# A Fourier mixer on folded tokens and channels: projecting, transforming and projecting back the even and the odd part separately

## The chip, the cores and the metric

The kernel runs on one core of a Trainium2 chip. The metric is the device time of one execution in microseconds. A core has five engines with their own instruction streams: TensorE (PE; matmuls, with weight loads shown as PEld), VectorE (DVE), ScalarE (ACT), GpSimd (POOL) and SyncE (SP, which issues most DMAs). Matmuls read SBUF and write PSUM; PSUM has eight banks of 512 fp32 columns.

## What is computed

One step of a small diffusion backbone with two layers. 512 latent tokens (a grid of 8 rows by 64 columns) and 128 context tokens, of 1024 channels each, share the weights. Each layer is a half-step SwiGLU feed-forward, a token mixer and a second half-step feed-forward, each wrapped in RMSNorm before and after, with shift, scale and gate from a modulation (`W_mod`) of a condition vector. The mixer of layer 1 is attention. The mixer of layer 0, which the change is about, is

```
def _fourier_mix(h, w_in, w_out):
    b, s, _ = h.shape
    u = (h @ w_in).reshape(b, s, N_FOURIER_GROUPS, FOURIER_GROUP_DIM)      # 8 groups of 128 channels
    f = jnp.fft.fft2(u.astype(jnp.float32), axes=(1, 3), norm="ortho").real
    return f.astype(h.dtype).reshape(b, s, D_MODEL) @ w_out
```

taken over the 512 latent tokens and over the 128 context tokens as two sequences. The real part of a two-dimensional transform is cosine times cosine minus sine times sine. A cosine sees only the even part of its input, the sum of a token (or channel) and its mirror image, and a sine only the odd part, the difference.

## The kernel before, in words

All matrices are fp32. A product is made of three matmuls (`mm3`, L233): each operand is split into a rounded part "hi" and a rest "lo" (`split`, L220: a copy on ACT, L222, and a subtraction on DVE, L223), and hi·hi, hi·lo and lo·hi are summed in PSUM (L236 to L238). Every weight unit, 128 x 1024, is loaded by SP into one of four "raw" buffers, split by ACT and DVE into one of six "hi"/"lo" pairs or into "ring" blocks, and used by PE; `unit` (L175) sends units three ahead of the one that is asked for.

The work is a sequence of six sub-layers n = 0 to 5. Feed-forward n = 0 (`ffn`, L624) goes over 22 hidden blocks in five slices: for each slice a w1 part (320-column matmuls over the two token halves) and a w2 part (512-column matmuls for five token tiles of 128, accumulated in PSUM and parked in SBUF between slices). In the last slice w2 runs over tiles (0, 1), then 2, then (3, 4). After a tile's last matmul `chain` (L567) does its post-norm, gate and residual (L576 to L586), the next pre-norm (L595 to L603), and then, a set number of modelled PE nanoseconds later (the number that the first `yield` hands out), eight PE transposes into channel-major form (L608), the scale and shift (L617 on ACT, L619 on DVE) and the split into the next layer's hidden state. The context is tile 4.

The modulation weights of later sub-layers are worked off in the background: 128 jobs, each one raw load and two DVE multiply-and-sum operations (L432). The list `BEHIND` says how many of them stand behind the w2 parts of each feed-forward (36 for n = 0); 12 jobs stand in the Fourier layer, six behind its input projection and six behind its output projection.

The Fourier layer (`fourier`, L964), n = 1:

- input projection: for each token half (320 tokens) eight output blocks of 128 channels times eight contraction chunks, `multi` (L273), copied into y channel-major (L1011);
- `fold` (L974, DVE): tokens and their mirror images are added and subtracted along the free axis;
- `channels` (L1018): per group of 128 channels, plain fp32 matmuls with the 128 x 128 cosine and sine matrices (L1026 to L1030), result split;
- `positions` (L1037): per group, three-matmul products with the 256-row position matrices (256 or 258 columns), then the unfolding of even and odd sums (L1049 to L1055) and a split;
- `out_proj` (L946): tiles (0, 1), then 2, then (3, 4), each tile two 512-column halves times eight chunks; tiles 0, 1 and 3 in the four "main" banks, tiles 2 and 4 in the two "score" banks. After each group the chains of its tiles start.

PSUM is handed out by tag: four "main" banks, two "score", one "turn", one "sum". A bank comes free when the last reader of its former tile is done.

## Time and profile before

| | us |
|---|---|
| median of 3 runs (lowest to highest) | 2217.96 (2216.83 to 2218.72) |
| profiled execution | 2217.38 |
| its span, first to last instruction | 2215.6 |
| PE busy in it | 2186.6 |
| DVE busy | 1724.0 |
| ACT busy | 1171.5 |
| POOL busy | 42.8 |

The rest of the profiled execution's time, 1.8 us, lies around the span. The page's groups name the line, the engine, the operation, "out<-in" by tile names, the shape, the count, and after the bar the busy time, the mean duration of one and the idle time of the engine just before it, with what ended that idle time. The view by stretches gives the same busy times for windows of the span. The timeline lists instructions in order of time with start and duration.

### The profile page before, as it was taken

To read this page: it belongs to the slowest core of one execution; us is meant where nothing else is said; L and a number is where in the kernel's file an instruction comes from. 1 tells how busy PE (TensorE), PEld (TensorE's weight loads), DVE (VectorE), ACT (ScalarE), POOL (GpSimd) and SP (SyncE) were. 2 spreads that over 40 slices of the span, in tenths; PEclk is the share of its full clock that TensorE was granted. 3 is DMA by queue.
4 is the path that set the end of the run, shared out by engine and by line. 5 is a ranking of instruction groups with operands and counts; after the bars stand their busy time and mean duration, and the time that the engine had idled before them with its cause. 6 is when DMAs were issued, how large, how long until landed. Compare 5 with 4: busy or idle time off the path is not lost. (4 is left out here: it accounts for less than half of the span.)

```text
span 2215.6 us, 35198 instructions
## 1 busy us (share of the span) xinstructions
PE 2186.6 (99%) x13646; PEld 2039.2 (92%) x13646; DVE 1724.0 (78%) x3158; ACT 1171.5 (53%) x2207; POOL 42.8 (2%) x95
## 2 busy tenths in 40 slices
PE   7999999999999999999999999999999999999998
PEld 5999998999899998998999999989999899999997
DVE  5988898687888898887988898786555686766684
ACT  4544544464454454455544554466778654455452
POOL 0000000000000000000000000000000000000000
PEclk9999999999999999999999999999999999999999
DMA  8244344533424444444244344523343322322232
GB/s 315 86 143 162 134 152 135 189 118 100 157 89 150 136 141 145 159 144 168 90 145 158 126 148 149 199 82 107 104 120 110 104 95 99 113 95 87 95 126 103
DMA packets 85575, 292.33 MB, mean 132 GB/s; under 512 B 9664, under 2 KB 14624, under 8 KB 85280
## 3 DMA queue, kind: packets, MB, share of 16 engines
q1 hardware_dynamic: 84864, 289.43, 38.9%
q8 instruction: 107, 1.75, 0.3%
q10 hardware_dynamic: 544, 0.66, 0.1%
q14 instruction: 60, 0.49, 0.1%
HBM read 274.53 MB, written 11.58 MB: 129 GB/s over the span
## 5 line engine op out<-in xcount | busy, mean ns | idle before, releaser
L222 ACT ACTIVATE hi<-raw 128x1024 fp32r<-128x1024 f32 (+1 forms) x387 | 369.2, 967 | 297.7 <-PE score L237 85.0
L223 DVE TENSOR_TENSOR lo<-raw,hi 128x1024 fp32r<-128x1024 f32 (+1 forms) x387 | 427.9, 1112 | 103.4 <-ACT hi L222 102.0
L236 PE MATMUL main<-hi,ring 128*128 128x512 f32 (+2 forms) x1044 | 391.9, 376 | 1.8 <-ACT ring L1338 1.8
L432 DVE SCALAR_TENSOR_TENSOR junk<-raw,wide 128x1024 bf16<-128x1024 f32 x256 | 313.2, 1223 | 97.1 <-DMA raw<-in_w_mod_t 92.5
L237 PE MATMUL main<-lo,ring 128*128 128x512 f32 (+2 forms) x1044 | 387.6, 371 | 0.8 <-DVE lo L223 0.8
L238 PE MATMUL main<-hi,ring 128*128 128x512 f32 (+2 forms) x1044 | 387.2, 371 | 0.0
L238 PE MATMUL score<-ring,lo 128*128 128x320 f32 x916 | 283.5, 309 | 0.8 <-DVE lo L223 0.6
L236 PE MATMUL score<-ring,hi 128*128 128x320 f32 x916 | 283.6, 310 | 0.0
L237 PE MATMUL score<-ring,hi 128*128 128x320 f32 x916 | 283.0, 309 | 0.0
L236 PEld LDWEIGHTS main<-hi,ring 128*128 128x128 f32 x1044 | 196.3, 188 | 36.7 <-ACT ring L1338 2.2
L238 PEld LDWEIGHTS main<-hi,ring 128*128 128x128 f32 x1044 | 196.0, 188 | 34.3 <-issue 0.2
L237 PEld LDWEIGHTS main<-lo,ring 128*128 128x128 f32 x1044 | 196.3, 188 | 33.4 <-DVE lo L223 1.1
L236 PE MATMUL turn<-ring,hi 128*128 128x320 f32 x680 | 210.8, 310 | 2.5 <-DVE left L760 2.5
L236 PE MATMUL sum<-ring,hi 128*128 128x320 f32 x680 | 210.4, 309 | 0.3 <-DVE left L764 0.3
L238 PE MATMUL turn<-ring,lo 128*128 128x320 f32 x680 | 210.1, 309 | 0.0
L237 PE MATMUL sum<-ring,hi 128*128 128x320 f32 x680 | 210.1, 309 | 0.0
L238 PE MATMUL sum<-ring,lo 128*128 128x320 f32 x680 | 210.1, 309 | 0.0
L237 PE MATMUL turn<-ring,hi 128*128 128x320 f32 x680 | 210.1, 309 | 0.0
L824 ACT ACTIVATE y<-main 128x512 f32<-128x512 f32 x160 | 94.1, 591 | 198.4 <-PE main L238 197.4
L236 PE MATMUL main<-ring,hi 128*128 128x320 f32 x560 | 181.5, 324 | 2.0 <-ACT ring L222 1.6
L238 PE MATMUL main<-ring,lo 128*128 128x320 f32 x560 | 175.1, 313 | 1.7 <-DVE lo L223 1.7
L237 PE MATMUL main<-ring,hi 128*128 128x320 f32 x560 | 174.9, 312 | 0.8 <-DVE ring L223 0.8
(253 smaller groups left out, 4292.5 us busy)
## 6 DMA issues: line engine op xcount, KB each, us to landing
raw<-in_w SPq DMA_DIRECT2D x272, 512.0 KB, 3.8
raw<-in_w_mod_t SPq DMA_DIRECT2D x128, 512.0 KB, 3.5
raw<-in_qkv SPq DMA_DIRECT2D x26, 512.0 KB, 3.7
spill<-ring SPq DMA_DIRECT2D x12, 640.0 KB, 3.0
ring<-spill SPq DMA_DIRECT2D x12, 640.0 KB, 6.7
raw<-in_bias SPq DMA_DIRECT2D x16, 448.0 KB, 3.5
first<-in_w_mod_k SPq DMA_DIRECT2D x8, 512.0 KB, 8.0
ring<-in_w_mod_k SPq DMA_DIRECT2D x8, 512.0 KB, 10.2
```

Of the source, the lines that this page charges most:

```text
L222: a = self.nc.scalar.activation(hi, src, AF.Copy)
L223: self.last_split = a, self.nc.vector.tensor_tensor(lo, src, hi.bitcast(F32), op=ALU.subtract)
L236: mm(out, whi, xhi, start=start, stop=False)
L237: mm(out, whi, xlo, start=False, stop=False)
L238: self.latest = mm(out, wlo, xhi, start=False, stop=stop)
L432: last = self.nc.vector.scalar_tensor_tensor(out=self.junk, in0=raw, scalar=1.0, in1=self.wide[:, cond, :], op0=ALU.mult, op1=ALU.mult, ac ...
L824: nc.scalar.activation(place(i, a), ps[a], AF.Copy)
```

## The change

**Token order.** The host puts latent tokens and their mirror images into two tiles at the same rows: tiles 0 and 1 are a pair, tiles 3 and 4 are a pair, and the context becomes tile 2, in the order 0 to 64, then 127 down to 65. Input, outputs, bias, cache outputs and the column ranges in attention (`QUERY_SEGS`, `KEY_SEGS`, `ATT_SPAN`, `ATT_COLS`, `OUT_COLS`) follow it; attention's token halves become 256 and 384 columns.

**Folding.** In `chain` of n = 0 the two tiles of a pair are replaced by sum and difference before the transposes, which are done for both at once; the context tile is folded after them. The input projection's weights are folded over channels and the output projection's over channels when a unit is sent (`send`, kinds `fold` and `foldrows`).

**Fourier layer.** Input projection token-major: even tokens against even channels (2 x 260 columns), odd tokens against odd channels (504 columns); then positions (`sums`, `diffs`), then channels (with two groups in one 128 x 128 block matrix), then the output projection of even and odd part, added and subtracted into the two tiles of a pair. The order of the output is pair (0, 1), tile 2, pair (3, 4).

**Schedule.** `BEHIND` for n = 0 is 48 instead of 36, and the 12 jobs in the Fourier layer are gone. The delays before transposes for n = 0 are a list of their own. In feed-forward 0 the last slice takes tiles 3 and 4 one after the other, and tile 4 no longer starts in fresh "score" banks.

The diff, cut to its core:

```diff
-BEHIND = (36, 12, 36, 36, 0, 8)
+BEHIND = (48, 0, 36, 36, 0, 8)
+TURNS = (
+    {0: 10500, 1: 14000, 2: 9200, 3: 11000, 4: 13000},
+    {1: 15500, 2: 9200, 4: 12500},
+)
...
+        elif kind.startswith("fold"):
+            raw = self.raw_tile(src)
+            a, b = raw[:, one], raw[:, two]
...
+            nc.vector.tensor_tensor(b, a, b, op=ALU.subtract)
+            for x, y in [(a, b)] if "rows" in kind else [(a[:, i], b[:, i]) for i in range(2)]:
+                nc.vector.scalar_tensor_tensor(out=x, in0=x, scalar=2.0, in1=y, op0=ALU.mult, op1=ALU.subtract)
...
+            if pair:
+                a, b = (self.wide_y[:, j * D : (j + 1) * D] for j in pair)
+                tt(b, a, b, op=ALU.subtract)
+                nc.vector.scalar_tensor_tensor(out=a, in0=a, scalar=2.0, in1=b, op0=ALU.mult, op1=ALU.subtract)
...
-        yield {0: 10500, 1: 14000, 2: 9200, 3: 11000, 4: 13000 if (n + 1) % 3 != 1 else 15000}[i]
-        turned = [self.bank(kind) for kind in (("score", "score") if i > 2 else ("turn", "sum"))]
+        yield TURNS[n == 0][i]
...
-        fresh = {(end, 0)} if final else {(end, 0), (end, 4)}
+        single = final or n == 0
+        fresh = {(end, 0)} if single else {(end, 0), (end, 4)}
...
-                if layer == 0 and tiles[0] == 0 and k < 6:
-                    self.behind()
...
+        def even_in(k, x, es):
+            w = self.unit(base + k)
+            n = x[0].free_size()
+            for a in range(2):
+                cols = slice(260 * a, 260 * a + 260)
+                self.mm3(es[a][:n, :260], *x, w[0][:, cols], w[1][:, cols], k == 0, k == NCH - 1)
+
+        def odd_in(k, x, o):
+            w = self.unit(base + k)
+            self.mm3(o[: x[0].free_size(), :504], *x, w[0][:, 520:], w[1][:, 520:], k == 0, k == NCH - 1)
+
+        def pair_in(p):
+            es, o = [self.bank() for _ in range(2)], self.bank()
+            for k in range(NCH):
+                even_in(k, token(k, 256 * p, 256 * p + P), es)
+                odd_in(k, token(k, 256 * p + P, 256 * p + 256), o)
...
+        self.close(1)
+        rows = {0: pair_in(0)}
+        self.close(2)
+        odd = self.bank()
+        for k in range(NCH):
+            odd_in(k, token(k, LAT, LAT + 64), odd)
+        even = [self.bank() for _ in range(2)]
+        for k in range(NCH):
+            even_in(k, token(k, LAT + 64, TOK + 2), even)
...
+        self.close(4)
+        rows[1] = pair_in(1)
...
+        def sums(m):
+            ps = self.bank()
+            out = ps[: 8 if m == 4 else P, :322]
+            self.mm3(out, *(columns(t, m) for t in ends), even_w[0][:66, 516:838], even_w[1][:66, 516:838], True, False, True)
+            for j in range(2):
+                ws = slice(258 * j, 258 * j + 258)
+                self.mm3(out[:, 64:], *(columns(t, m) for t in rows[j]), even_w[0][:, ws], even_w[1][:, ws], False, j == 1, True)
...
+        def diffs(m):
...
+            for j in range(2):
+                ws = slice(256 * j, 256 * j + 256)
+                self.mm3(out[:, P:], *(t[:, 520:][:, us] for t in rows[j]), odd_w[0][:, ws], odd_w[1][:, ws], j == 0, j == 1)
+            self.latest = mm(out[:, :P], plain[:, us], small[:64, :P], start=True, stop=True)
...
+        def channels(m, p, q):
+            ps = self.bank("score")[:, :322]
+            self.mm3(ps, mid_w[0][:, :P], mid_w[1][:, :P], *p, True, False)
+            for i in range(2):
+                self.latest = mm(ps, odd_w[0][:8, 512 + P * m : 640 + P * m], middle[i], start=False, stop=i == 1)
+            for i in range(2):
+                mm(x5, mid_w[0][:, 256 + 72 * m : 328 + 72 * m], p[i], start=m == i == 0, stop=False)
+            self.split(*even_at(m, 0, 322), ps)
+            ps = self.bank("score")[:, :384]
+            self.mm3(ps, mid_w[0][:126, P : 2 * P], mid_w[1][:126, P : 2 * P], *q, True, True)
+            self.split(*odd_at(m, 0, 384), ps)
...
+        def pair_out(p):
+            near, far = [], []
+            for a in halves:
+                near.append(self.bank())
+                far.append(self.bank())
+                for m in range(4):
+                    w = self.unit(at + 4 * a + m)
+                    self.mm3(near[a], *even_at(m, 66 + P * p, P), w[0][:, :WIDE], w[1][:, :WIDE], m == 0, False)
+                    self.mm3(far[a], *odd_at(m, P + P * p, P), w[0][:, WIDE:], w[1][:, WIDE:], m == 0, m == 3 and p == 1, not p)
...
+            with high():
+                for a in halves:
+                    copy(ts[a], near[a], AF.Copy)
+                for a in halves:
+                    stt(out=near[a], in0=far[a], scalar=k[1], in1=ts[a], op0=ALU.mult, op1=ALU.add)
+                for a in halves:
+                    stt(out=far[a], in0=ts[a], scalar=k[0], in1=far[a], op0=ALU.mult, op1=ALU.add)
+            boundary(i, near)
+            boundary(j, far)
...
+        own = [self.bank("score") for _ in halves]
+        for a in halves:
+            even_out(a, 0, 66, own[a])
...
+        pair_out(0)
+        ctx = [self.bank(kind) for kind in ("turn", "sum")]
+        for a in halves:
+            odd_out(a, 0, ctx[a])
...
+        boundary(2, ctx)
+        pair_out(1)
```

`even_out` and `odd_out` are loops like those in `pair_out` over four units each; `even_out` ends with one matmul for the middle channel.

More of the change, by code (lines that the diff above doesn't have):

```diff
@@ L105, in chunk @@
     def chunk(self, c, half):
+        if self.width > TOK:
+            return tuple(self.tokens(part, c, *ATT_SPAN[half]) for part in range(2))
         return self.at(0, c, half)[:, 0, :], self.at(1, c, half)[:, 0, :]
@@ L606, in chain @@
+        yield TURNS[n == 0][i]
+        tiles = pair or (i,)
+        kinds = [("turn", "sum"), ("score", "score")]
+        if i > 2 and not pair:
+            kinds.reverse()
+        turned = [[self.bank(kind) for kind in kinds[j]] for j in range(len(tiles))]
         with self.tc.issue_after(self.latest.ins):
-            for c in range(NCH):
-                nc.tensor.transpose(turned[c // 4][:, c % 4 * P : (c % 4 + 1) * P], place[:, c * P : (c + 1) * P], self.ident)
+            for banks, j in zip(turned, tiles):
+                for c in range(NCH):
+                    at = self.wide_y[:, j * D + c * P : j * D + (c + 1) * P]
+                    nc.tensor.transpose(banks[c // 4][:, c % 4 * P : (c % 4 + 1) * P], at, self.ident)
@@ L845, in ffn @@
             elif op == "w2":
-                for tiles in ((3,), (4,)) if final and a[1] == (3, 4) else (a[1],):
+                for tiles in ((3,), (4,)) if single and a[1] == (3, 4) else (a[1],):
                     w2(a[0], tiles)
@@ L992, in zero @@
-        def zero(g0):
-            ps = self.bank("sum")
-            nc.tensor.matmul(ps[:, :8], cos, self.y[:, g0 : g0 + 4, 0 : LAT + 1 : LAT], start=True, stop=True)
-            c = self.col(8)
-            v = ps[:, :8].rearrange("p (g t) -> p g t", t=2)
-            cc = c.rearrange("p (g t) -> p g t", t=2)
-            nc.scalar.activation(cc[:, :, 0], v[:, :, 0], AF.Copy, scale=LAT ** -0.5)
-            nc.scalar.activation(cc[:, :, 1], v[:, :, 1], AF.Copy, scale=CTX ** -0.5)
-            for i in range(4):
-                first[g0 + i] = (c[:, 2 * i : 2 * i + 1], c[:, 2 * i + 1 : 2 * i + 2])
@@ L1003, in fourier @@
-        for half in (0, 1):
-            lo, hi = SPAN[half]
-            self.finish(half)
-            for m0 in (0, 4):
-                kinds = ("main",) * 4 if half or m0 else ("main", "main", "turn", "sum")
-                pss = self.multi([self.unit(base + m) for m in range(m0, m0 + 4)], half, kinds)
-                with self.tc.high_priority():
-                    for m, ps in zip(range(m0, m0 + 4), pss):
-                        nc.scalar.activation(self.y[:, m, lo:hi], ps[:, :HALF], AF.Copy)
-                if half and not m0:
-                    fold(m0, nc.vector)
-                self.behind((0, 3, 3, 0)[2 * half + m0 // 4])
@@ L1059, in fourier @@
-        channels(0)
-        fold(4, nc.vector)
-        for g in range(NCH):
-            if g + 1 < NCH:
-                channels(g + 1)
-            positions(g)
-        self.out_proj(0, base + NCH + 2, boundary)
+        nc, h = self.nc, self.h
+        copy, tt, mm = nc.scalar.activation, nc.vector.tensor_tensor, nc.tensor.matmul
+        stt = nc.vector.scalar_tensor_tensor
+        high = self.tc.high_priority
+        small = self.temp("right")[:, :208]
+        nc.sync.dma_start(out=small, in_=self.io["dft_small"])
@@ new lines, in fourier @@
+        self.close(1)
[7 more added lines that the diff above has]
+            even_in(k, token(k, LAT + 64, TOK + 2), even)
+        plain, ends = self.ring(F32)[:64, :504], self.ring(F32R)
+        ends = ends[:66, :520], ends[:66, 520:1040]
+        with high():
+            copy(plain, odd[:64, :504], AF.Copy)
+            for a in range(2):
+                self.split(ends[0][:, a * 260 : a * 260 + 260], ends[1][:, a * 260 : a * 260 + 260], even[a][:66, :260])
@@ new lines, in fourier, with positions @@
+        self.split(*middle, sums(4))
+        xe = [self.wide_ring(F32R) for _ in range(2)]
+        yo = [[self.ring(F32R) for _ in range(2)] for _ in range(2)]
+        last = self.ring(F32R)[:72, :322]
+        x5 = self.bank("sum")[:72, :322]
+        even_at = lambda m, lo, n: [t[:, 322 * m + lo : 322 * m + lo + n] for t in xe]
+        odd_at = lambda m, lo, n: [t[:, 384 * (m % 2) + lo : 384 * (m % 2) + lo + n] for t in yo[m // 2]]
+        def positions(m):
+            ps = sums(m)
+            p = [self.temp("left", F32R)[:, :322] for _ in range(2)]
+            self.split(*p, ps)
+            ps = diffs(m)
+            q = [self.temp(kind, F32R)[:126, :384] for kind in ("square", "total")]
+            self.split(*q, ps)
+            return p, q
```

380 lines of the change are left out of this document (244 added, 136 removed).

## The prediction, on record before the run

> **What bounds the kernel now.** I read the page first: one engine is busy for nearly the whole span.
>
> ```profile
> span 2215.6 us, 35198 instructions
> PE 2186.6 (99%) x13646; PEld 2039.2 (92%) x13646; DVE 1724.0 (78%) x3158; ACT 1171.5 (53%) x2207; POOL 42.8 (2%) x95
> ```
>
> So the time is TensorE's (PE's) work, and the question is how much of it the change takes away and whether VectorE (DVE) can keep up afterwards. That can only be seen by stretches. The next view gives busy us and the number of instructions of PE, PEld, DVE, ACT and POOL, in this order, then granted clock, DMA share and GB/s. The stretches are: feed-forward 0 from its first w2 pass to the start of its last, one w1 part of it, that last pass, then the Fourier layer's input projection, transform and output projection, and last 200 us of attention.
>
> ```profile
> 104.40:424.50 320.10, 319.29 (x1912) 299.59 (x1911) 280.87 (x462) 155.92 (x246) 0.00 (x0) 1.00 0.44 146
> 131.60:181.00 49.40, 49.35 (x336) 49.05 (x336) 46.61 (x79) 24.40 (x38) 0.00 (x0) 1.00 0.42 139
> 424.50:468.00 43.50, 43.50 (x206) 36.29 (x205) 29.46 (x64) 25.25 (x63) 3.23 (x6) 1.00 0.34 126
> 468.00:526.40 58.40, 58.39 (x402) 58.07 (x401) 41.08 (x74) 21.97 (x45) 2.12 (x4) 1.00 0.48 161
> 526.40:552.20 25.80, 25.80 (x213) 23.13 (x212) 22.57 (x59) 17.45 (x46) 0.00 (x0) 1.00 0.14 45
> 552.20:609.70 57.50, 57.50 (x267) 47.58 (x266) 49.63 (x97) 28.80 (x63) 3.20 (x6) 1.00 0.47 158
> 1500.00:1700.00 200.00, 198.84 (x1642) 193.86 (x1642) 111.48 (x368) 149.25 (x397) 8.11 (x24) 1.00 0.36 108
> ```
>
> PE has no holes from 104.4 to 609.7 us, 505.3 us in all, at full clock. DVE is busy for 280.87 + 29.46 + 41.08 + 22.57 + 49.63 = 423.6 us of them, a share of 0.838; in feed-forward 0 it is 0.877, and in the w1 part 46.61 / 49.40 = 0.944 with PE still full. These three shares decide the forecast.
>
> **PE's part: the price of a matmul.** A matmul's duration overlaps the next one, so its price is the distance of two starts in the timeline.
>
> ```profile
> 519.83 0.31 PE L236 MATMUL main<-ring,hi 128*128 128x320 f32 x1
> 519.97 0.31 PE L237 MATMUL main<-ring,hi 128*128 128x320 f32 x1
> 520.12 0.31 PE L238 MATMUL main<-ring,lo 128*128 128x320 f32 x1
> ...
> 528.33 0.39 PE L1027 MATMUL score<-ring,ring 128*128 128x128 f32 x2
> 528.55 0.39 PE L1026 MATMUL score<-ring,y 128*128 128x128 f32 x2
> ...
> 529.36 0.28 PE L237 MATMUL main<-lo,ring 128*128 128x258 f32 x1
> 529.57 0.32 PE L1029 MATMUL turn<-ring,y 128*64 128x128 f32 x1
> ...
> 530.16 0.28 PE L237 MATMUL main<-lo,ring 128*128 128x256 f32 x1
> 530.28 0.28 PE L236 MATMUL main<-hi,ring 128*128 128x258 f32 x1
> ...
> 570.26 0.39 PE L236 MATMUL main<-ring,ring 128*128 128x512 f32 x1
> 570.49 0.39 PE L237 MATMUL main<-ring,ring 128*128 128x512 f32 x1
> 570.71 0.39 PE L238 MATMUL main<-ring,ring 128*128 128x512 f32 x1
> ```
>
> 320 columns cost 0.145 us (0.29 over two), 512 cost 0.225 (0.45 over two), 256 cost 0.12, and a plain fp32 matmul of 128 columns, two records, 0.22. Between the sizes I take a straight line: 0.122 for 258 and 260, 0.147 for 322, 0.173 for 384, 0.223 for 504.
>
> Before: 2 halves x 8 outputs x 8 chunks x 3 = 384 matmuls of 320 are 55.7 us, the transform 25.8, and 5 tiles x 2 x 8 x 3 = 240 of 512 are 54.0. With 40 transposes at about 0.1 these are the three windows, 141.7 us; without the transposes, which stay, 137.7.
>
> After, input: per pair of tiles and chunk 6 matmuls of 260 (even part) and 3 of 504 (odd part), 16 times: 11.7 + 10.7; the context's odd rows 24 x 0.223 = 5.4 and even rows 48 x 0.122 = 5.9. Sum 33.7. Transform: five position sums of 3 x 0.147 + 6 x 0.122 = 5.9; four differences of 6 x 0.12 + 0.22 = 3.8; four channel steps of 7 x 0.147 + 3 x 0.173 = 6.2; the last two 0.3. Sum 16.2. Output: 26 + 100 + 24 = 150 matmuls of 512 are 33.8, and two fp32 matmuls of 512 columns (four times the 0.22) 1.8. Sum 35.6. Together 85.5: 52 us less.
>
> The narrow shapes (64, 8 or 4 output columns, 64, 8 or 2 contracted rows) go in and out of the full array some 26 times. The rows show such a change: from a 258 matmul to a 64-column one 0.21 us pass instead of 0.12, so 0.09 each, 2.4 us in all; a narrow shape does nothing the full one doesn't, so no gain, and at most twice this. The Trainium skill's page "TensorEngine Tiling (Array Packing)", section Key Properties, says that a change of tiling mode drains the engine; the 0.21 us agrees that something is paid, and if each change cost a whole drain of at most the 0.28 us that such a matmul lasts, its sum would be an estimated 7 us and not 2.4. PE alone thus gives back 52 - 2 = 50 us.
>
> **DVE's part: is there room?** The rows are groups of DVE operations from 420 to 620 us (count | busy us, mean ns | idle).
>
> ```profile
> L432 DVE SCALAR_TENSOR_TENSOR junk<-raw,wide 128x1024 bf16<-128x1024 f32 x24 | 29.4, 1224 | 15.2 <-DMA raw<-in_w_mod_t 14.9
> L223 DVE TENSOR_TENSOR lo<-raw,hi 128x1024 fp32r<-128x1024 f32 x23 | 27.8, 1222 | 3.9 <-ACT hi L222 3.7
> L223 DVE TENSOR_TENSOR ring<-y,ring 128x256 fp32r<-128x256 f32 x24 | 8.8, 421 | 0.0
> L223 DVE TENSOR_TENSOR ring<-y,ring 128x512 fp32r<-128x512 f32 x12 | 8.0, 688 | 0.6 <-ACT ring L222 0.6
> L223 DVE TENSOR_TENSOR ring<-score,ring 128x512 fp32r<-128x512 f32 x8 | 5.5, 682 | 0.0
> L1051 DVE TENSOR_TENSOR y<-left,main 128x256 f32<-128x256 f32 x8 | 3.4, 421 | 3.4 <-ACT left L1049 3.4
> L1052 DVE TENSOR_TENSOR y<-left,main 128x252 f32<-128x252 f32 x8 | 3.3, 409 | 0.0
> L1055 DVE SCALAR_TENSOR_TENSOR ring<-main,col,ring 128x128 fp32r<-128x128 f32 x8 | 2.7, 343 | 0.0
> L576 DVE TENSOR_TENSOR score<-score,y 128x512 f32<-128x512 f32 x4 | 2.7, 700 | 10.2 <-PE score L238 10.2
> L983 DVE TENSOR_TENSOR ring<-y 128x1008 f32<-128x1008 f32 x2 | 2.4, 1202 | 0.0
> ```
>
> Out of the Fourier stretch go: the 12 modulation jobs, 24 x 1.22 = 29.4; the token fold, four times 1.2 and about 2 of small pieces; the two kinds of splits, 8 x 0.68 and 8 x 0.69 = 11; the unfold, 3.4 + 3.3 + 2.7 and 2.4 of tiny copies; tile 4's two accumulator adds, 1.4. Sum 60.
>
> In come, priced by size from the same rows: the weight folds, 8 x (0.69 + 2 x 0.41) = 12.1 for the input units and 8 x 2 x 0.69 = 11 for the output units; one more unit split, 1.2; two pairs of tiles folded, 4 x 1.22 = 4.9; the context's fold and single columns, 2.2; splits of the projections, 3.9; splits of sums, differences and channels, 4 x 2 x (0.49 + 0.56) + 0.9 = 9.3; the parting of the outputs, 10 x 0.7 = 7. Sum 52. The 29.4 us of the modulation jobs aren't gone: they move into feed-forward 0, behind four w2 slices instead of under the projections.
>
> So from 104.4 us to the end of the Fourier layer DVE has 423.6 - 60 + 52 + 29.4 = 445 us to do, while PE's own need falls from 505.3 to 455. PE could only run free if DVE were busy 0.98 of the time, and no stretch above shows that. **The gain is cut by DVE, and the length of this stretch is DVE's work over the share it can reach.** The share seen with PE full is 0.944; much of the new work isn't background but sits in chains with PE, ACT and POOL. I take 0.935, just under it: 445 / 0.935 = 476 us, 29 us shorter than 505.3.
>
> As a second way to the same number, the places where PE would wait:
>
> ```profile
> 471.81 1.41 DVE L586 SCALAR_TENSOR_TENSOR ring<-main,col,ring 128x512 f32<-128x512 f32 x2
> ...
> 575.93 1.65 DVE L586 SCALAR_TENSOR_TENSOR ring<-main,col,ring 128x256 f32<-128x256 f32 x4
> ...
> 579.82 1.41 DVE L586 SCALAR_TENSOR_TENSOR ring<-main,col,ring 128x512 f32<-128x512 f32 x2 [0.54 <-POOL col L564]
> ```
>
> (a) Input projection of the first pair, 9 us (2 to 14). Its odd part needs a third "main" bank, and all four belong to tiles 3 and 4; the projection starts at 468.0 and the last-tile chain lets its banks go when L586 ends, 5 us later. At the same time DVE owes the four units still to fold and split (4 x 2.7), tile 3's and 4's chains and the pair's evacuation, while PE would eat a unit per 1.4 us. Behind the waiting matmul stands all of PE's queue.
> (b) Entry to the transform and its steps, 3 us (0 to 8): the first sum needs both splits of the last projection, ACT and DVE one after the other; the work that could cover is three matmuls.
> (c) Output of the second pair, 4 us (1 to 8). It needs the four main banks of the first pair. Today tile 0's are read out by 577.6 and tile 1's by 581.2, some 7 us after these tiles' last matmul (552.3 + 96 x 0.225 = 573.9); the parting adds two copies and four operations, so the last comes free after about 10 us, and the context's 24 x 0.225 = 5.4 us is all that covers it.
> (d) Feed-forward 0, 5 us (0 to 15): six more modulation operations of 1.22 us in each slice of 76 us, of which DVE has about 9 us idle.
>
> These are 21 us, so 50 - 21 = 29 us of gain, the same as by the share.
>
> **Behind it**, 2.5 us lost (0 to 6). Attention's matmuls are split 256 + 384 instead of 320 + 320, which is 0.12 + 0.173 against 0.29: nothing. It gains small copies, some 16 on ACT, which at the 0.34 us of L1055 (128 columns, on DVE) are 5 us, where ACT is busy 149 of 200 us and waits on nobody for long. The second feed-forward's first half needs the context tile, now computed 11 us before it instead of 18.
>
> DMA sends one unit and one small matrix more; at a share of at most 0.48 in every stretch above I cost it nothing.
>
> **The sum**, against the profiled execution: 2217.38 us, of which 2215.6 are the span, and the median of the runs is 2217.96. 2217.4 - 29 + 2.5 = **2191 us**.
>
> **Rivals.**
> 1. *PE's count is the whole story*: DVE packs to 0.97, and the waits (a) to (c) fall into each other. Then 2217.4 - 50 + 1 = 2168 us. For it: DVE's 0.944 cost PE nothing. Against: twice the latency chains in two thirds of the time. Chance 0.17.
> 2. *DVE reaches only 0.90*, a little over what feed-forward 0 shows: 445 / 0.90 = 494.4, so 2217.4 - 10.9 + 2.5 = 2209 us. Chance 0.2.
> 3. *Slower: DVE becomes the bound from 104 us on and keeps its present share.* At 0.838 the stretch lasts 531 us and the whole 2217.4 + 25.7 + 2.5 = 2246 us. It decides as soon as the share is below 445 / 507 = 0.878, the 0.877 of feed-forward 0 today. For it: in both stretches DVE already idles for data (10.2 us for PE, 14.9 for the modulation weights' DMA), and the moved jobs are those that wait for DMA. Against: 0.944 in the w1 part. Chance 0.06.
>
> My forecast, a share of 0.92 to 0.96 and so 2178 to 2198 us, keeps 0.57. The range is 2166 to 2210 us: it takes in most of rivals 1 and 2 and leaves out their outer ends and rival 3, some 0.2. A measurement here can tell about 0.2%, 4.4 us: below 2213 lie the forecast, rival 1 and most of rival 2, 0.91; within 4.4 us 0.03; above, 0.06.
>
> **What would show it.** Right: the Fourier layer's PE work is 86 to 89 us without transposes; PE idle of 10 to 25 us appears, most of it in the first pair's projection and before the second pair's output; DVE's share from 104 us to the layer's end is 0.92 to 0.96; attention and later stages keep their lengths within 3 us. Wrong: PE idle in feed-forward 0 of over 10 us (rival 3 begins), or no new idle at all (rival 1), or a matmul of 260 or 504 columns that does not lie on the line through 0.145 and 0.225.

## The result: slower by 1.4%

| | before | after |
|---|---|---|
| median (lowest to highest), us | 2217.39 (2215.16 to 2218.72) | 2249.03 (2245.7 to 2250.7) |
| span of the profiled execution, us | 2215.6 | 2247.6 |

The ratio of after to before is 1.0142, with a 95% interval of 1.0124 to 1.0159. The forecast of 2191 us had the wrong sign. The page of the changed kernel, its first lines and the clock in 40 slices:

```profile
span 2247.6 us, 34637 instructions
PE 2173.4 (97%) x13299; PEld 1999.0 (89%) x13299; DVE 1753.9 (78%) x3255; ACT 1175.2 (52%) x2222; POOL 44.4 (2%) x95
PEclk9999999998989999999999999999999999999999
```

PE has 347 matmul records fewer, but is busy for only 13 us less, waits more, and the clock has two dents. The stretches that answer to those of before (columns as there; the second row is one w1 part, rows four to six are the mixer's three steps, the last of them up to the first matmul of feed-forward 1):

```profile
104.70:460.50 355.80, 333.88 (x1912) 308.01 (x1912) 310.36 (x516) 155.73 (x245) 0.00 (x0) 0.97 0.45 149
132.60:189.50 56.90, 51.55 (x336) 50.39 (x335) 52.04 (x89) 24.32 (x38) 0.00 (x0) 0.97 0.45 148
460.50:504.90 44.40, 44.40 (x206) 36.13 (x205) 34.07 (x75) 23.50 (x60) 4.77 (x8) 1.00 0.25 94
504.90:554.10 49.20, 40.80 (x234) 33.80 (x233) 39.12 (x78) 22.91 (x53) 1.13 (x2) 0.86 0.39 125
554.10:575.40 21.30, 20.51 (x124) 16.59 (x123) 18.16 (x31) 11.83 (x23) 0.00 (x0) 1.00 0.34 107
575.40:629.40 54.00, 40.26 (x177) 29.21 (x175) 42.21 (x78) 35.98 (x77) 6.52 (x10) 0.90 0.36 128
```

Feed-forward 0 ends at 504.9 instead of 468.0 us (+36.9), though its matmuls are hardly touched. The mixer takes 124.5 us instead of 141.7 (17.2 less; PE is busy in it for 40 us less, but 22.9 us of waits appear). The rest, to the end of the span, takes 1618.2 us instead of 1605.9 (+12.3). That is the whole difference of the spans, 32.0 us. What PE waited for between 104 and 630 us (sum, times, longest), where before there was one wait of 0.7 us:

```profile
PE score L274 <- ACT hi L260: 12.2, 4, 4.0
PE turn L665 <- DVE y L644: 11.8, 1, 11.8
PE main L275 <- DVE lo L261: 7.2, 2, 6.7
PE score L276 <- DVE lo L261: 5.2, 3, 4.4
PE score L274 <- ACT left L856: 4.3, 3, 1.4
PE main L274 <- ACT ring L260: 2.2, 2, 1.4
PE main L274 <- DVE ring L627: 1.2, 1, 1.2
```

In these rows the arrow points at what ended the wait. The "score" rows are feed-forward 0, the "main" rows the mixer, "turn <- y" the start of feed-forward 1. A wait costs more than its length. PE's timeline behind one of them:

```profile
154.46 0.49 PE L274 MATMUL score<-ring,hi 128*128 128x320 f32 x1 [3.78 <-ACT hi L260]
154.75 0.47 PE L275 MATMUL score<-ring,hi 128*128 128x320 f32 x1
155.02 0.47 PE L274 MATMUL turn<-ring,hi 128*128 128x320 f32 x1
...
158.34 0.31 PE L276 MATMUL turn<-ring,lo 128*128 128x320 f32 x1
158.49 0.31 PE L274 MATMUL turn<-ring,hi 128*128 128x320 f32 x1
```

For 3.5 us after a wait of 3.78 us the starts lie 0.27 us apart and not 0.147: the granted clock is 0.5. In the w1 part of the second row PE is idle for 5.4 us, and the part is 7.5 us longer than before. The Trainium skill, page "TensorE: Matmul & The Clock Gate", section "What's actually happening", says that the array falls to half rate after an idle window of about 3.4 us and needs as long a busy one to come back; the waits of 3.8 us and more here agree, with spells of 3.4 to 13.7 us behind them, while those of 1.4 us in the same parts were followed by none. A whole window without work was not needed, though, and there the measurement decides: the changed kernel's clock is also 0.5 for 3.4 us from 509.6 us on, behind waits of 0.6 and 1.2 us, and both kernels have such a spell at 39 us behind a wait of 1.7 us.

Three theories came out of this comparison. **Jobs:** the 12 modulation jobs that the change moves behind feed-forward 0 make PE wait there. **Blocks:** the ring's blocks became eight columns (32 bytes) wider, to 5,152 bytes, for the mixer's wider operands, and every 512-column matmul with a stationary block of the ring (the operand that is loaded into the array as weights; the other one moves through it) is dearer. **Turns:** the waits in and behind the mixer are the fixed order of VectorE's instructions and not its amount of work. The rival to the last, and the forecast's own picture, is that VectorE's work over the share it can reach sets the time.

### The profile page after: what moved, and what is told of

Same layout as the page of the kernel before. It is cut to its first block, busy times and chain, and to the rows that moved or that the text cites. A ratio compares the mean times of both kernels' runs of the same rounds, so it can differ in the third digit from the quotient of the medians.

```text
span 2247.6 us, 34637 instructions
## 1 busy us (share of the span) xinstructions
PE 2173.4 (97%) x13299; PEld 1999.0 (89%) x13299; DVE 1753.9 (78%) x3255; ACT 1175.2 (52%) x2222; POOL 44.4 (2%) x95
## 4 chain that ended last, share of the span: by engine, by line
PE 82%; DVE 9%; DMA 4%; ACT 3%; issue 2%; POOL 0%; SPq 0%; DVEq 0%; POOLq 0%; ACTq 0%
PE main L274 11%; PE main L275 11%; PE main L276 11%; PE score L274 7%; PE score L276 7%; PE score L275 7%; PE turn L274 4%; PE turn L275 4%; PE turn L276 4%; PE sum L276 4%; PE sum L275 4%; PE sum L274 4%; DVE junk L473 3%; DMA raw<-in_w_mod_t 2%; DVE lo L261 2%
## 5 line engine op out<-in xcount | busy, mean ns | idle before, releaser
L260 ACT ACTIVATE hi<-raw 128x1024 fp32r<-128x1024 f32 (+1 forms) x388 | 370.8, 968 | 291.5 <-PE score L275 88.6
L261 DVE TENSOR_TENSOR lo<-raw,hi 128x1024 fp32r<-128x1024 f32 (+1 forms) x388 | 429.2, 1113 | 105.2 <-ACT hi L260 103.6
L275 PE MATMUL main<-lo,ring 128*128 128x512 f32 (+5 forms) x1089 | 408.8, 376 | 8.1 <-DVE lo L261 8.1
L274 PE MATMUL main<-hi,ring 128*128 128x512 f32 (+4 forms) x1089 | 411.1, 379 | 2.0 <-DVE ring L627 1.2
L276 PE MATMUL main<-hi,ring 128*128 128x512 f32 (+5 forms) x1089 | 407.8, 375 | 0.0
L274 PE MATMUL score<-ring,hi 128*128 128x320 f32 x916 | 287.3, 314 | 16.6 <-ACT hi L260 12.2
L275 PE MATMUL score<-ring,hi 128*128 128x320 f32 x916 | 286.0, 312 | 0.0
L275 PEld LDWEIGHTS main<-lo,ring 128*128 128x128 f32 (+2 forms) x1089 | 204.7, 188 | 47.2 <-DVE lo L261 9.2
L274 PEld LDWEIGHTS main<-hi,ring 128*128 128x128 f32 (+2 forms) x1089 | 203.7, 188 | 43.6 <-DVE ring L627 1.4
L276 PEld LDWEIGHTS main<-hi,ring 128*128 128x128 f32 (+2 forms) x1089 | 204.6, 188 | 40.0 <-issue 0.6
L274 PE MATMUL sum<-ring,hi 128*128 128x320 f32 x672 | 207.5, 309 | 0.3 <-DVE left L868 0.3
L275 PE MATMUL sum<-ring,hi 128*128 128x320 f32 x672 | 207.7, 309 | 0.0
L274 PEld LDWEIGHTS score<-ring,hi 128*128 128x128 f32 x916 | 175.0, 191 | 19.9 <-ACT hi L260 13.4
L276 PEld LDWEIGHTS score<-ring,lo 128*128 128x128 f32 x916 | 174.6, 191 | 8.1 <-DVE lo L261 8.1
L275 PEld LDWEIGHTS score<-ring,hi 128*128 128x128 f32 x916 | 175.2, 191 | 0.7
```

What stands on the lines that cost most here:

```text
L260: a = self.nc.scalar.activation(hi, src, AF.Copy)
L261: self.last_split = a, self.nc.vector.tensor_tensor(lo, src, hi.bitcast(F32), op=ALU.subtract)
L274: mm(out, whi, xhi, start=start, stop=False)
L275: mm(out, whi, xlo, start=False, stop=False)
L276: self.latest = mm(out, wlo, xhi, start=False, stop=stop)
```

## Experiments

### The moved jobs: b48 and spread

b48 is the kernel before, with nothing of the change but the jobs' place:

```
-BEHIND = (36, 12, 36, 36, 0, 8)
+BEHIND = (48, 0, 36, 36, 0, 8)
...
-                if layer == 0 and tiles[0] == 0 and k < 6:
-                    self.behind()
...
-                self.behind((0, 3, 3, 0)[2 * half + m0 // 4])
```

> The kernel before with one part of the change alone: 48 modulation jobs behind the w2 parts of feed-forward 0 and none in the Fourier layer. Theory 1 (the 12 moved jobs are what lengthened feed-forward 0): each of the four w1 parts after a w2 part grows from 49 to about 57 us with 5 us of PE idle and a spell of half clock, the Fourier layer gains nothing because PE bounds it, and the time is 2217 + 33 = 2250 us (2240 to 2255). Rival (another part of the change, such as the token order or the wider blocks, lengthened it): 2217 us within 3.

Measured: 2256.53 us against 2218.38, ratio 1.0174 (1.0159 to 1.0189), 1.5 us above the range of the theory and far from its rival. Its waits in feed-forward 0:

```profile
PE score L236 <- ACT hi L222: 13.1, 6, 4.0
PE score L238 <- DVE lo L223: 7.2, 5, 5.4
PE score L236 <- ACT left L752: 4.3, 3, 1.4
```

They are nearly the changed kernel's, at the same instructions. The jobs alone cost 38 us; the mixer without them took the same 58 us for its input projection, so nothing came back. Why so much? In the changed kernel, SP and VectorE around the third of the parts:

```profile
295.80 10.63 SPq L201 DMA_DIRECT2D raw<-in_w_mod_t  x6
309.14 9.44 SPq L201 DMA_DIRECT2D raw<-in_w  x3
```

```profile
303.58 1.22 DVE L473 SCALAR_TENSOR_TENSOR junk<-raw,wide 128x1024 bf16<-128x1024 f32 x1
...
317.00 1.22 DVE L473 SCALAR_TENSOR_TENSOR junk<-raw,wide 128x1024 bf16<-128x1024 f32 x1
...
318.95 1.22 DVE L261 TENSOR_TENSOR lo<-raw,hi 128x1024 fp32r<-128x1024 f32 x1
```

Six loads of modulation weights stand on SP's queue ahead of the next units' and fill the four raw buffers; VectorE works the jobs off one after the other until 318, and only then makes the rest part (L261) that PE is waiting for. In the other three parts PE waits 3.8 to 4.0 us for a rounded part on ScalarE (L260), and that for sums on VectorE (L226 to L228) which stand behind the jobs in the same way. Between jobs and PE's supply nobody chooses: the order is fixed. The w2 part didn't take them either. It holds 14 of the jobs' operations in both kernels, and VectorE idles there for 5 us, each time for the next modulation weights; the surplus falls into the first 15 to 19 us of each w1 part. The idle time of VectorE in one w2 part, then its job operations in one w1 part, before and in the changed kernel:

```profile
  DMA raw<-in_w_mod_t: 5.2, 3
  DMA raw<-in_w_mod_t: 5.1, 3
```

```profile
L432 DVE SCALAR_TENSOR_TENSOR junk<-raw,wide x5: 1216/1219/1224, 208.4 to 214.4; 128x1024 bf16<-128x1024 f32 x5
L473 DVE SCALAR_TENSOR_TENSOR junk<-raw,wide x11: 1218/1222/1226, 301.8 to 317.0; 128x1024 bf16<-128x1024 f32 x11
```

spread is the changed kernel with the jobs given back: 36 behind feed-forward 0, four ahead of its last output slice, four behind the first pair's projection, four ahead of the first pair's output.

```
+                if n == 0 and a[0] == end and a[1] == (0, 1):
+                    self.behind(4)
         rows = {0: pair_in(0)}
+        self.behind(4)
...
+        self.behind(4)
         pair_out(0)
```

> The changed kernel with 36 jobs behind the w2 parts of feed-forward 0 as before, and the 12 others where its trace shows DVE idle: 4 behind the start of the last slice's w2, 4 after the first pair's input projection, 4 before the first pair's output. Theory 1: feed-forward 0's w1 parts are 49 to 50 us again, 33 us less, and the jobs cost 0 to 8 us in the holes: 2216 to 2224 us. Rival (DVE is the bound all the way and the jobs cost the same wherever they stand): 2240 us or more.

Measured: 2237.45 us, ratio 1.0088 (1.0071 to 1.0104), between the theory's range and the rival's. Feed-forward 0 has no wait left, but the start of feed-forward 1 has a new one:

```profile
609.69 1.11 PE L665 MATMUL turn<-ident,y 128*128 128x128 f32 x4 [21.75 <-ACT y L686]
```

The last four jobs carry the shift and scale of feed-forward 1. VectorE reached them between 594 and 608 us, behind the output's chains, and the copies of L686 need their result. The mixer, with 8 of the 12 jobs, now takes 140 us. The four w1 parts, from the first matmul's start to the last's, are as long as before again (49.0, 49.1, 49.0 and 61.6 us, in the changed kernel 56.9, 57.3, 58.0 and 71.2), so the 33 us by which these grew are shown to be the jobs; and the jobs have a price wherever they stand too late.

### The ring's blocks: bring8, aring16, p128, shift128, even

bring8 is the kernel before with blocks eight columns wider, unused:

```
-        return self.blkp.tile([P, 2 * TOK], dt, tag="blk", ...)
+        return self.blkp.tile([P, 2 * TOK + 8], dt, tag="blk", ...)[:, : 2 * TOK]
```

> The kernel before with one part of the change alone: every ring block is 8 columns (32 bytes per partition) wider, the extra columns unused; the ones tile, which nothing reads, is left out to make room. Theory 2 (the block pitch of 5152 bytes instead of 5120 slows matmuls whose weights come from ring blocks): a 512-column matmul of the w2 parts takes 0.233 instead of 0.227 us, some 3100 of them 0.006 us each, so 2217 + 19 = 2236 us (2230 to 2238). Rival (the 0.233 comes from traffic of the background jobs or the new layer): 2217 us within 3, matmuls at 0.227.

Measured: 2231.9 us, ratio 1.0065 (1.005 to 1.008), 13.5 us for a change that computes nothing. aring16 and p128 are the changed kernel with `2 * TOK + 16` and `2 * TOK + 32` columns, and with a smaller modulation table (p128 with an 8-bit scrap tile as well) to make room in SBUF; aring32, the same blocks as p128 without that room, did not fit and gave no time.

> The changed kernel with the ring's blocks 32 bytes further apart (5,184 bytes in place of 5,152; the modulation sums of the two layers share one table to make the room). Theory of the pitch: it is the 32 byte offset of every second block against 64 that slows the 512-column multiplications whose stationary operand lies in the ring, from 0.2268 to 0.2329 us; with 5,184 bytes they come back to 0.227 and the kernel loses 13 to 16 us, to 2,233 to 2,236 us. Rival: only the old 5,120 bytes are right for them (or the longer ring as such is wrong); they stay at 0.232 to 0.233 us and the time at 2,246 to 2,251 us. Nothing else should move: the first parts of feed-forward 0 stay at 57 us with 5 us of idle TensorE each.

Measured: 2247.3 us, ratio 1.0135 (1.012 to 1.015): the rival.

> The changed kernel with the ring's blocks 5,248 bytes apart (41 times 128; room from a smaller modulation table and an 8-bit scrap tile). 5,184 bytes did not bring the 512-column multiplications back to 0.227 us. Theory: what counts is a distance that is a multiple of 128 bytes: 0.227 us again and 13 to 16 us less than the changed kernel, 2,233 to 2,236 us. Rival: only multiples of 512 (5,120 was one) do, or something else than the distance: 0.231 to 0.233 us and 2,245 to 2,251 us.

Measured: 2241.33 us, ratio 1.0102 (1.0087 to 1.0118): halfway. The answer was in this run, once its matmuls were sorted by the addresses that the kernel gives its tiles: where the stationary block and the moving tile start alike modulo 256 bytes, starts lay 227 to 228 ns apart, where they differ by 128 bytes, 233 ns. A test of that theory moves no size, only a start; the kernel before gets a gap of 128 bytes ahead of the ring:

```
+        pool("gap", 1).tile([P, 32], F32, name="gap")
         self.blkp = pool("blk", NBLK)
```

> The kernel before with 128 unused bytes ahead of the ring: blocks still 5,120 bytes apart, but each starts 128 bytes (mod 256) off from the tiles of the moving operand, where both started alike. Theory that the start of the stationary block against the moving one within 256 bytes decides (with blocks 5,248 apart, those that agreed took 0.227 to 0.228 us and those 128 off 0.233 us): all 512-column multiplications with a stationary block of the ring go from 0.227 to 0.233 us, 12 to 17 us more than before, 2,229 to 2,235 us. Rival: the distance of 5,120 is what is good; 0.227 us and 2,215 to 2,221 us.

Measured: 2231.11 us, ratio 1.0059 (1.0043 to 1.0076), as the theory had it. One w2 part each: before has its row for the same 120 matmuls first, shift128 the second, the changed kernel the third, and even, below, the last.

```profile
104.40:131.60 27.20, 27.20 (x122) 22.54 (x121) 21.23 (x35) 10.32 (x17) 0.00 (x0) 1.00 0.42 142
```

```profile
104.60:132.50 27.90, 27.90 (x122) 22.67 (x122) 22.51 (x36) 10.32 (x17) 0.00 (x0) 1.00 0.42 141
```

```profile
104.70:132.60 27.90, 27.90 (x122) 22.48 (x122) 22.54 (x35) 10.41 (x17) 0.00 (x0) 1.00 0.40 139
```

```profile
104.00:131.20 27.20, 27.20 (x122) 22.53 (x121) 20.51 (x35) 10.32 (x17) 0.00 (x0) 1.00 0.42 142
```

PE never waits in any of them; 128 bytes of offset cost 0.7 us in 27.2. even undoes it in the changed kernel: blocks 5,248 bytes apart, and those in the odd places used from byte 128 on.

```
-        return self.wide_ring(dt)[:, : 2 * TOK]
+        return self.slot(dt)[:, 32 * (SHIFTED >> self.slots & 1) :][:, : 2 * TOK]
```

> The changed kernel with blocks 5,248 bytes apart and every second one used from its byte 128 on, so that nearly every stationary block starts alike (mod 256) with the moving operand. Theory of the start: the 512-column multiplications take 0.227 us as in the kernel before, 13 to 15 us less than the changed kernel, 2,234 to 2,237 us, where p128 (every second block alike) had 0.230 us and 2,241.3. Rival: 0.229 us and more, 2,239 to 2,243 us.

Measured: 2236.72 us, ratio 1.0088 (1.0073 to 1.0103), 12.3 us less than the changed kernel. It has p128's smaller tables too; aring16, with one of them, gained nothing clear of noise, and a job operation took 1.22 us with the 8-bit scrap tile as without. This term is settled in both directions. The 320-column matmuls, which move ring blocks and hold the weights still, kept their 0.147 us throughout. Why a start within 256 bytes matters was not tried further; aring16 shows that it isn't the whole rule, since blocks that started alike took 230 ns there.

### The start of feed-forward 1: order and act

In the changed kernel the root that tile 2's scaling (L644) needs was there at 615.1 us, and the scaling came at 624.4, behind the parting of the second pair and what follows it:

```profile
613.70 1.39 POOL L605 TENSOR_TENSOR col<-col,power 128x1 f32<-128x1 f32 x1 [6.47 <-DVE col L602]
624.43 0.75 DVE L644 TENSOR_SCALAR y<-ring,col 128x1024 f32<-128x1024 f32 x1
```

order changes that turn alone (cut to the one line):

```
-            with high():                                            # pair_out's parting
+            with high(), self.behind_of(*self.scaled if p else []):  # behind tile 2's L644
```

> The changed kernel with one thing alone: the parting of the second pair of output tiles is issued behind the row scaling of tile 2. Theory of the turn: the 11.8 us for which TensorE waits at the start of feed-forward 1 are the turn of tile 2's scaling in VectorE's fixed order (ready at 615.1, run at 624.4 us); issued first, the wait falls to 1 to 4 us and the half clock behind it goes too: 9 to 14 us less, 2,235 to 2,240 us. Rival: the wait is the work itself (root, scaling, transposition and parting of tile 2 cannot be quicker), or tiles 0 and 1 come late in its place: less than 3 us, 2,246 to 2,250 us.

Measured: 2242.42 us, ratio 1.0115 (1.0099 to 1.013), 6.6 us less than the changed kernel and between the two ranges. Its PE timeline there:

```profile
613.05 0.63 PE L667 MATMUL turn<-ident,y 128*128 128x128 f32 x4 [1.29 <-DVE y L644]
613.51 0.60 PE L667 MATMUL sum<-ident,y 128*128 128x128 f32 x4
618.97 0.63 PE L274 MATMUL turn<-ring,hi 128*128 128x320 f32 x1 [4.86 <-ACT ring L260]
```

The wait of 11.8 us was the turn, as expected. What comes next was not expected: the copies and splits of that tile then keep PE waiting 4.9 us, against 1.4 before, so a third of the 10.5 us is taken back. act gives the copies of the turned tiles, ahead of the mixer and of feed-forward 1, all to ScalarE:

```
-                    if c < 4:
+                    if c < (NCH if n < 2 else 4):
```

> The changed kernel with the copies of the turned tiles out of their banks (before the mixer and before feed-forward 1) all on ScalarE, in place of half on VectorE: VectorE loses 40 operations of 0.34 us, 14 us, and ScalarE gains as many of 0.36 us. Theory that VectorE's work bounds these places: the waits of 6.7 us in the first pair's projection and of 11.8 us at the start of feed-forward 1 shrink together by 5 to 14 us, 2,235 to 2,244 us. Rival: the waits are chains (root, scaling, transposition, copy, parting) in which ScalarE's copies come one after the other: no gain, or up to 5 us slower, 2,247 to 2,254 us.

Measured: 2242.31 us, ratio 1.0107 (1.0092 to 1.0122): 6.7 us less, inside the first range. It shortens both waits (6.7 to 3.5 and 11.8 to 3.9 us). That fits less VectorE work and fits a shorter piece ahead of the awaited one; nofold tells these apart.

### The mixer: pool, nofold, turn34

pool moves the subtraction of each weight fold to the idle GpSimd (`nc.vector.tensor_tensor` to `nc.gpsimd.tensor_tensor`).

> The changed kernel with the first step of each weight fold (the subtraction, 16 times 0.68 us on VectorE, 11 us in all) on GpSimd, which is idle in the Fourier mixer. Theory that VectorE's work bounds the mixer's input projection: the wait of 6.7 us in the first pair's projection shrinks or goes and the mixer is 5 to 11 us shorter than its 124.5 us, 2,238 to 2,244 us in all; feed-forward 0 stays as it is. Rival: the subtraction takes GpSimd much longer (from its 0.46 us for 64 by 128 elements, some 1.8 us for 512 columns) and each unit comes later by that, so that nothing is gained: 2,248 to 2,256 us.

Measured: 2257.21 us, ratio 1.0176 (1.0159 to 1.0193), 8 us slower than the changed kernel and 1 above the rival's range. A subtraction took GpSimd 1.34 us (median of 16) against 0.68 on VectorE, and the wait in the first pair's projection grew from 6.7 to 7.2 us. Nothing is said by it about VectorE's load, as each unit also came later. nofold leaves the folds out altogether, and with them that part of the computation:

```
-            nc.vector.tensor_tensor(b, a, b, op=ALU.subtract)
-            for x, y in ...:
-                nc.vector.scalar_tensor_tensor(out=x, in0=x, scalar=2.0, in1=y, ...)
```

> The changed kernel without the folds of the mixer's weights (it leaves that part of the computation out: 16 subtractions and 24 to 32 scaled ones, some 23 us of VectorE's work around and in the mixer). Theory that VectorE's work holds the mixer at 124.5 us: 10 to 20 us less, the 6.7 us wait in the first pair's projection gone, 2,229 to 2,239 us. Rival: the chains from the tiles to the multiplications hold it: under 5 us less, 2,244 to 2,249 us. The waits in feed-forward 0 and the 11.8 us at the start of feed-forward 1 should not move under either.

Measured: 2250.98 us, ratio 1.0149 (1.0134 to 1.0164): no gain at all, 2 us above the rival's range. What PE waits for in the mixer, and the first pair's projection by stretch:

```profile
PE turn L662 <- DVE y L641: 11.8, 1, 11.8
PE main L272 <- DVE lo L258: 7.3, 2, 6.7
```

```profile
503.40:552.00 48.60, 39.18 (x237) 33.17 (x236) 32.38 (x61) 24.12 (x55) 1.13 (x2) 0.93 0.39 130
```

VectorE is busy 0.67 of this step instead of 0.80, and the same two waits are there, 6.7 us in it and 11.8 us at the start of feed-forward 1. For the mixer the forecast's picture, work over a reachable share, falls with this run. VectorE in the changed kernel during the 6.7 us:

```profile
516.89 0.87 DVE L682 TENSOR_SCALAR y<-score,coef 128x128 f32<-128x128 f32 x3 [0.20 <-PE score L665]
517.76 1.37 DVE L688 TENSOR_SCALAR y<-sum,coef,sk 128x128 f32<-128x128 f32 x4
519.04 0.34 DVE L682 TENSOR_SCALAR y<-score,coef 128x128 f32<-128x128 f32 x1
519.53 3.66 DVE L261 TENSOR_TENSOR ring<-y,ring 128x256 fp32r<-128x256 f32 x13
523.10 1.22 DVE L261 TENSOR_TENSOR lo<-raw,hi 128x1024 fp32r<-128x1024 f32 x1
```

Copies and splits of a pair of tiles run in one piece, and the rest part of the weight unit that PE needs next comes last. turn34 lets tiles 3 and 4 ask 6.5 us later (`TURNS`: 12500 to 19000 for tile 4).

> The changed kernel with one number changed: the pair of tiles 3 and 4 asks for its transposition 6.5 us later (of the order's own clock), so that its copies and splits, some 6 us of VectorE in one piece, stand behind the splits of the first pair's last weight blocks. Theory of the turn: the 6.7 us wait in the first pair's projection falls under 2 us, and the half clock behind it (10 us) goes: 5 to 10 us less, 2,239 to 2,244 us, unless the second pair's projection now waits for the same piece. Rival: the piece only moves, and the wait comes at the second pair's projection: 2,246 to 2,252 us.

Measured: 2247.35 us, ratio 1.0124 (1.0102 to 1.0147), inside the rival's range and not clear of the changed kernel. The wait stayed where it was and fell to 4.3 us: the second pair's fold and the first tiles' splits now stand in the same place. That turns decide is shown for the start of feed-forward 1; for this wait it is shown that the weight folds don't, and that moving the second pair's piece takes 2.4 us off it. The rest stays open.

### Together: combo, combo2, combo3b, combo3c, combop, combo5

All have 36 to 40 jobs behind feed-forward 0, order's edit, four jobs behind the first pair's projection and one behind each step of the transform (`self.behind(1)`), so that the last coefficients come early enough.

> The changed kernel with three edits together: the blocks 5,184 bytes apart; tile 2's scaling before the parting of the second pair; and 36 modulation jobs behind feed-forward 0 as in the kernel before, with 4 more before its last output slice, 4 behind the first pair's input projection and one behind each of the four steps of the transform, early enough for the next feed-forward. Theory that the loss is the sum of three mechanisms: feed-forward 0 back to some 468 us, the 512-column multiplications at 0.227 us, no wait over 4 us at the start of feed-forward 1, and 5 to 15 us of waits in the mixer, since VectorE does 29 us more there: 2,195 to 2,212 us, under the 2,218 us of the kernel before. Rival: VectorE's work up to the end of the mixer is what bounds, wherever the jobs stand, and what feed-forward 0 gains the mixer loses: 2,220 to 2,235 us.

Measured: 2222.84 us, ratio 1.0024 (1.0015 to 1.0033), inside the rival's range. Feed-forward 0 is back, 37 us shorter than in the changed kernel, and the mixer lost 7.5 of these (132.0 instead of 124.5), so the rival's number came without its reason. The blocks aren't back (5,184 bytes), and the mixer's longest waits are 4.7, 5.0, 3.1, 2.7 and 3.0 us.

> Combo (36 jobs behind feed-forward 0, tile 2 scaled first) with blocks 5,248 bytes apart and all copies of the turned tiles on ScalarE. If both theories hold, 2,222.8 less 12 us for the blocks and less 5 to 12 us for VectorE's relief in the mixer: 2,199 to 2,206 us, under the kernel before by some 0.7%. If neither holds: 2,220 to 2,227 us, and the folded mixer pays nothing with these prices.

Measured: 2220.76 us, ratio 1.0016 (1.0006 to 1.0025), inside the second range.

> Combo2 with the jobs placed once more: 40 behind feed-forward 0 (ten a slice in place of nine), none before its last output slice, four behind the first pair's input projection and one behind each step of the transform. Theory of a full VectorE: a slice has room for one more job (it is 0.93 busy there and a job takes 2.4 of 49.1 us), so that feed-forward 0 gets at most 1 to 3 us longer, while the wait of 5.3 us at the mixer's start and the half clock behind it go: 2,211 to 2,218 us. Rival: the tenth job makes TensorE wait in each slice as the three more jobs of the change did, in proportion 8 to 12 us: 2,220 to 2,230 us.

Measured: 2223.28 us, ratio 1.0029 (1.0014 to 1.0043), inside the rival's range. The wait at the mixer's start went from 5.3 to 2.3 us, and the tenth job of a slice cost feed-forward 0 some 5 us, with waits up to 2 us in three parts: the gain was paid back.

> Combo3b with the scaling of the rows ahead of the mixer and of feed-forward 1 on ScalarE too (nine operations, 0.75 us each on VectorE, some 1.05 us on ScalarE). If VectorE's work still sets the waits in the mixer: 3 to 7 us less than combo3b. If by now the chains of the tiles do (each gets 0.3 us longer and ScalarE is fuller): no change or up to 4 us slower than combo3b.

Measured: 2231.68 us, ratio 1.0066 (1.0044 to 1.0088), 8 us slower than combo3b. Less work for VectorE made it worse than either expectation: the waits at the start of feed-forward 1 went from 2.5 and 2.7 to 4.9 and 5.4 us, ScalarE being the one they end with.

> Combo with blocks 5,248 bytes apart and nothing else (the copies of the turned tiles on both engines as in the changed kernel). From combo's 2,222.8 us and the 5.7 us by which those blocks beat the ones 5,184 apart in the changed kernel: 2,215 to 2,219 us, level with the kernel before. If the copies on ScalarE were a help in combo2, it is slower than combo2's 2,220.8 us.

Measured: 2222.16 us, ratio 1.0016 (1.0007 to 1.0026). Not the 2215 to 2219; its ratio is combo2's, so the copies on ScalarE are neither help nor harm once tile 2 goes first. Starts of 512-column matmuls lay 230.6 ns apart on the mean against combo's 231.3, half the step from aring16 (231.5) to p128 (230.1); the rest of the miss was not located.

> The repairs together: blocks as in even, 38 jobs behind feed-forward 0, two before its last output slice, four behind the first pair's input projection, one behind each step of the transform; tile 2 scaled first; copies of turned tiles on ScalarE. From combo2's 2,220.8: less 6 us for the blocks, and 0 to 5 us less for the jobs: 2,210 to 2,216 us, 0.1 to 0.3% under the kernel before. If the placing of the jobs gives back what the blocks give: 2,217 to 2,221 us.

Measured: 2213.14 us, ratio 0.9982 (0.9972 to 0.9992). It lies inside the first range and beats both kernels: the changed one by 1.6% and the one before by 0.18%, about what a measurement here can tell. Its feed-forward 0, last output slice, mixer up to the output, and output, then one row of its waits:

```profile
104.70:426.80 322.10, 319.92 (x1913) 299.68 (x1912) 289.58 (x480) 155.32 (x245) 0.00 (x0) 1.00 0.45 150
426.80:471.10 44.30, 43.73 (x207) 36.18 (x206) 30.14 (x63) 23.61 (x66) 4.31 (x8) 1.00 0.28 106
471.10:547.60 76.50, 63.42 (x343) 51.84 (x343) 64.48 (x117) 38.30 (x86) 1.12 (x2) 0.87 0.43 145
550.40:604.00 53.60, 43.40 (x177) 30.60 (x175) 42.90 (x76) 36.68 (x82) 4.55 (x7) 0.89 0.45 156
```

```profile
PE main L279 <- DVE ring L632: 5.4, 2, 3.1
```

The folded mixer now takes 132.9 us, 8.8 less than before, with eight jobs in it, against the 50 us that the forecast took from its multiplications. In the row of L632 the longest wait, 3.1 us up to 578.8, is the second pair's output waiting for the first pair's "main" banks, which the prediction listed under (c).

## Why the prediction was wrong

**Where the 58 us went.** Feed-forward 0 grew by 36.9 us and not by 5; the mixer gave 17.2 us and not 34 (50 less the waits (a) to (c)); behind it 12.3 us were lost and not 2.5. That is 32, 17 and 10 us.

**The step that failed is (d), "Feed-forward 0, 5 us (0 to 15)".** It came to 33 us in the w1 parts (b48: 38 us). The step set six more operations against 9 us of idle VectorE in a slice. But 5 of those 9 us lie in the w2 part, where VectorE idles because the next modulation weights aren't there yet; it took no more jobs. All six landed in the first third of a w1 part whose share of 0.944 left 2.8 us, ahead of the splits that PE needs. And a wait of 4 us brings the half clock with it. The sign named for this, PE idle in feed-forward 0 of over 10 us, came: 21.9 us.

**PE's prices held, the sum did not.** Matmuls of 260 and 504 columns lay on the line (0.12 and 0.23 us). But the mixer's PE time went from 141.7 to 101.6 us, against a predicted 92 (85.5 + 2.4 and 4 of transposes). Of these 9.6 us some 4.5 are half clock (17 matmuls of 504 columns at 0.41 us, ten of 260 at 0.25) and 1 the dearer 512-column matmuls; the rest was not located. On the side of before, the listed prices add up to 139.5 us and not to 141.7, so 2 of the predicted 52 us were never there by these prices.

**DVE's work held, the share didn't, and the share was the wrong idea.** The forecast was 445 us of work from 104 us to the mixer's end; the rows above give 310.36 + 34.07 + 39.12 + 18.16 + 42.21 = 443.9. The share was 0.846 and not 0.935. In the w1 part it fell from 0.944 to 0.915 (52.04 of 56.9 us) while PE began to wait, so it was not a bound that was reached; in the mixer nofold took VectorE's work away and gained nothing. A share that came out low was a sign of waits, not their cause. Rival 3, at 0.838, gave 2246 us, 3 us from the result, and that is luck: VectorE's work didn't set the time. One of its reasons was right, that the moved jobs are those that wait for DMA.

**A term was left out:** the blocks' start, 12.3 us in even. By the rows above some 4 of them are matmul time in feed-forward 0 (five w2 passes, 0.7 to 1 us each), 1 in the mixer (150 matmuls, 6 ns each), and 7 lie behind it (1618.2 us in the changed kernel, 1610.8 in even). In even's profiled execution the first 4 don't show in the time: its w1 parts are 4.6 us longer. Nothing in the profile of before shows the term; the diff does, as a changed size of a buffer that every stage uses. "Behind it, 2.5 us" was 12.3 with these 7. Most of the other 5 can be found in even: the first part of feed-forward 1, which begins at half clock, takes 69.4 instead of 66.9 us, and attention with the last w2 slice ahead of it 359.2 instead of 355.6.

**The waits.** (a) was 9 and is 8.4 us (0.6, 1.2 and 6.7), the third bank being the 1.2 of it (L627); the size was right, but most of it was the rest part that VectorE made last, and not the bank. (b) was 3 and is 0.8. (c) was 4 and didn't occur: the context's 24 matmuls, from 594.3 to 600.0 us, covered it. In combo5, where all but two of them ran earlier, it is there. The largest wait, 11.8 us for tile 2, was not on the list: "computed 11 us before it instead of 18" was read as room, when VectorE's order let tile 2 wait 9 us with its input ready.

## What to carry to other kernels

Idle time of an engine is room only for work whose data are there at that moment: see what ended each idle stretch before moving work into it, and follow the load queue and the buffers that the moved work shares with the critical supply. When a buffer changes size, check where every tile behind it now starts. And of a busy engine ask not only how much it does but what stands ahead of the one operation that is awaited; the folds' 15 us of VectorE's time, taken away elsewhere in the mixer, bought nothing.

## What the runs showed of the hardware

- A 512-column matmul whose stationary operand starts 128 bytes (modulo 256) off from its moving one took 0.233 instead of 0.227 us, 13 us in 2218 (shift128). The Trainium skill, page "SBUF — State Buffer", section "Operand start alignment", asks only for a multiple of the element size and says that its runs timed nothing; here is a time.
- The granted clock fell to half within a working kernel behind every wait of 3.8 us and more between 104 and 630 us of the changed kernel, and behind some of 1.2 to 1.7 us: 67.5 us at half clock in its profile, against 14.7 before.
- GpSimd took 1.34 us for a subtraction of 128 by 504 or 512 that takes VectorE 0.68.
